# Attention scores from half-array products, two key blocks' tiles at a time

## The chip, the core and the metric

The program runs on one core of a Trainium2 chip. The core has five engines that work through queues of their own in program order and meet at semaphores: TensorE (PE; the loading of its stationary operand is shown apart as PEld), VectorE (DVE), ScalarE (ACT), GpSimd (POOL) and SyncE (SP, which issues most transfers). The metric is the device time of one execution in microseconds, as the median of several. Lower is better.

## The reference, cut to what matters

One layer: a combined input projection of 2048 positions, then dilated attention in three head groups, a gated linear recurrence, two gated output projections, a merge, an output projection and a layer norm. The change lies in the attention.

```python
DILATION_GROUPS = ((128, 1), (512, 4), (2048, 16))     # (window, dilation); 8 heads of 64 each
...
    s = jnp.einsum('brnqhd,brnkhd->brnhqk', qb, kw) * (Dh ** -0.5)
    # query blocks of 128 against [previous block, current block] of keys, banded
    s = jnp.where(valid[None, None, :, None], s, NEG_INF)
    m = jnp.max(s, axis=-1, keepdims=True)
    p = jnp.exp(s - m)
    l = jnp.sum(p, axis=-1, keepdims=True)
    o = jnp.einsum('brnhqk,brnkhd->brnqhd', p, vw)
```

Everything is float32. The kernel multiplies in a reduced float32 type and restores the accuracy by splitting an operand x into a rounded high part and a low part, x - high; a product q k is formed as qh kh + ql kh + qh kl.

## The kernel before, in words

The program has three stages one after the other. The first (to 1464 us of the profiled execution) is the input projection; it writes the rotated queries, already split (`qh`, `ql`), and the keys to scratch in DRAM, channel by channel: 64 channels of one head on 64 partitions. The second (1464 to 1791 us) is the attention. The third is the combination of the groups and the other projections. The order on PE, ACT, DVE, POOL and SP is that in which the Python code emits the instructions; no scheduler moves them.

The attention loop runs over 192 tiles `m`, 16 in each of 12 units `u`. A unit is two heads of one group; the groups alternate in the order 0, 2, 1, dilations 1, 16, 4. A tile is one block of 128 queries for both heads, against one or two blocks of keys: a full tile has two key blocks (256 columns), a narrow one has one (128). Dilation 16 has narrow tiles only, dilation 4 has four narrow ones at the start of a unit, dilation 1 has one.

In step `m` of the loop the code emits three things for three different tiles:

- `step_s(m)`: the scores into PSUM (`s`), then on DVE, for each head, one instruction that adds the mask and takes the minimum (the signs are turned, so the minimum is the greatest score), and on ACT, for each head, the exponential (`p`);
- `step_t(m - 3)`: TensorE transposes the exponentials into PSUM (`pt`), and ACT or, for every third tile, DVE copies them to SBUF (`ptb`);
- `step_v(m - 4)`: TensorE multiplies the copied tile by the values (`o`); after every second tile DVE copies `o` to `osb`, which ACT's queue sends to DRAM.

For the scores, `unit_parts` lays queries and keys out so that 128 rows of the array are used for a head of 64 channels. `A[:, h]` holds the high queries on 64 partitions and the low ones on the other 64; `B1[:, h]` holds the high keys on both halves; `b2[:, h]` holds the low keys on the half of the high queries and zeros on the other. Two products per head then give all three terms. The keys are split on POOL when they have landed: a cast to the high part, a second cast that copies it to the other half, and a subtraction, for each head and each half of the positions (twelve instructions per unit, those of the first keys on ACT and DVE). A unit's keys and queries are asked for from SP during the unit before.

Names in the listings: `A` queries, `B` high keys, `C` keys and then their low part, `V` values, `k_scr`, `qh_scr`, `ql_scr`, `v_scr` the scratch they come from. The weights of the first stage are `l` (low parts, from `wl_scr`).

Of the kernel before, what the change touches and what calls it, by code (L numbers as in the profile page):

```python
# [15 lines left out]
P = 128  # L16
# [15 lines left out]
def hybrid_block_kernel(ctx: ExitStack, tc: tile.TileContext, a: dict, out: bass.AP):  # L32
# [634 lines left out]
    for s in range(1, NQ):  # L667
# [16 lines left out]
        for j in range(7):  # L684
            if plan[s][0] and j % 2 == 0:
                at(t0 + j - 1, lambda s=s, j=j: load_lo(s, j))
            at(t0 + j, lambda s=s, j=j: prep_w(s, j))
# [71 lines left out]
    USLOT = (("X4", "X3", "X2"), ("Y0", "X1", "X0"))  # L759
    VSLOT = {(0, 0): "X5", (2, 0): "Y1", (1, 0): "Y2", (0, 1): "X5", (2, 1): "Y1", (1, 1): "Y2"}  # L760
    zero = [False, False]
    B2 = {}
# [7 lines left out]
    def unit_parts(u):  # L770

        sl = USLOT[u % 2]
        g, hp = unit(u)
        q = {(n, h): qk_scr[n, 4 * g + hp].rearrange("(d h) s -> h d s", h=2)[h] for n in ("qh", "ql", "k") for h in range(2)}

        def k_part(h, hs, os):
            def fn():
                if h == 0:
                    units[u] = [None, big(sl[1], [P, 2, S], F32R, f"B{u}")]
                    if u < 2:  # L780
                        B2[u] = big(sl[2], [P, 2, S], F32R, f"C{u}")
                        pool.memset(flat(B2[u][up_, 0]), 0.0)
                        pool.memset(flat(B2[u][lo_, 1]), 0.0)
                    units[u].append(B2[u % 2])
                _, B1, b2 = units[u]
                sp.dma_start(flat(b2[hs, h]), q["k", h])

                def split(t):
                    if (u, h) == (0, 0):
                        act.activation(B1[hs, h, t], flat(b2[hs, h, t]), AF.Copy)  # L790
                        act.activation(B1[os, h, t], flat(B1[hs, h, t]), AF.Copy)
                        eng = dve
                    else:
                        pool.tensor_copy(B1[hs, h, t], flat(b2[hs, h, t]))
                        pool.tensor_copy(B1[os, h, t], flat(B1[hs, h, t]))
                        eng = pool
                    eng.tensor_tensor(out=b2[hs, h, t], in0=flat(b2[hs, h, t]), in1=flat(B1[hs, h, t]), op=ALU.subtract)  # L797

                later(3, lambda: split(slice(0, S // 2)))
                later(4, lambda: split(slice(S // 2, S)))  # L800
            return fn

        def q_part(hs, h, n):
            def fn():
                if (hs, h) == (lo_, 0):
                    units[u][0] = big(sl[0], [P, 2, S], F32R, f"A{u}")
                sp.dma_start(flat(units[u][0][hs, h]), q[n, h])
            return fn

        return [k_part(0, lo_, up_), k_part(1, up_, lo_), q_part(lo_, 0, "qh"), q_part(up_, 0, "ql"),  # L810
                q_part(lo_, 1, "ql"), q_part(up_, 1, "qh")]
# [66 lines left out]
    first, second, firstv = unit_parts(0), unit_parts(1), v_parts(0, 0)  # L878
    low = NS
    where = [(s, j) for s in range(NQ) for j in range(ticks[s])]  # L880
    for T, (s, j) in enumerate(where):
# [10 lines left out]
        if s == NQ - 1:  # L892
            for fn in ((), (), first[:2], first[2:], firstv, second[:1], second[1:2])[j]:
                fn()
        evacuate(s, j)
# [31 lines left out]
    def step_s(m):  # L927
        u, n = divmod(m, 16)
        g, _ = unit(u)
        A, B1, b2 = units[u]  # L930
        pv = prev(g, n)
        lo = 0 if pv is not None else P
        s = aps.tile([P, 2, 256], F32, tag="s", name=f"s{m}", bufs=3)
        if n % 4 == 0:
            st["osb"] = at_p.tile([P, 4, 132], F32, tag="osb", name=f"osb{m}", bufs=6)
        osb = st["osb"]
        for h in range(2):
            q = A[:, h, n * P:(n + 1) * P]
            for i, B in enumerate((B1, b2)):
                if g == 2:  # L940
                    k = B[:, h].rearrange("p (c r i) -> p r c i", c=4, r=16)[:, max(n - 1, 0):n + 1]
                elif pv is None:
                    k = B[:, h, n * P:(n + 1) * P]
                elif g == 0:
                    k = B[:, h, (n - 1) * P:(n + 1) * P]
                else:
                    c, r = divmod(n, 4)
                    k = B[:, h, (c - 1) * CH:(c + 1) * CH].rearrange("p (c r j) -> p r c j", c=2, r=4)[:, r]
                pe.matmul(s[:, h, (0 if g == 2 and n else lo):256], q, k, start=(i == 0), stop=(i == 1))  # L949
        p = at_p.tile([P, 2, 256], F32, tag="p", name=f"p{m}", bufs=5)  # L950
        for h in range(2):
            mm = osb[:, n % 4, 130 + h:131 + h]
            dve.tensor_tensor_reduce(out=p[:, h, lo:256], in0=s[:, h, lo:256], in1=mask[:, lo:256],  # L953
                                     scale=1.0, scalar=3e38, op0=ALU.add, op1=ALU.min, accum_out=mm)
            act.activation(p[:, h, lo:256], p[:, h, lo:256], AF.Exp, scale=-1.0, bias=mm)  # L955
# [87 lines left out]
    for m in range(NB + 4):  # L1043
        u, n = divmod(m, 16)
        run(late)
        if m < NB:
            step_s(m)
# [342 lines left out]
```

## Time and profile before

| | us |
|---|---|
| median of 3 runs | 2276.87 (2275.35 to 2277.63) |
| the profiled execution | 2272.4 |
| its span, first to last instruction | 2270.6 |
| first stage | 0 to 1464 |
| attention | 1464 to 1791 |
| the rest | 1791 to 2270.6 |

A row of busy time by stretches gives the stretch, its length and then for each engine the microseconds in which it was busy, with the number of instructions, then the granted TensorE clock (1.00 is full speed), the share of the DMA engines and GB/s. A row of the timeline gives start, duration, engine, line, operation, tiles written and read, and in brackets how long the engine had been idle and what ended that. A row of instruction groups gives line, engine, operation, tiles, shapes and count, then busy microseconds and mean nanoseconds of one, then the engine's idle time before them and what ended it. Matmuls overlap, so distances between their starts tell more than their durations.

### The profile page before, as it was taken

How to read it: one execution, taken by the hardware profiler on the slowest of the kernel's cores; microseconds unless marked ns; L12 is line 12 of the kernel's file. 1: busy time of each engine (PE TensorE's matmuls, PEld its weight loads, DVE VectorE, ACT ScalarE, POOL GpSimd, SP SyncE). 2: the span in 40 equal slices, each digit the busy share in tenths (PEclk: the TensorE clock that was granted, in tenths of full speed). 3: DMA queues.
4: the chain of work that ended last, by engine and by line, in shares of the span. 5: the costliest groups of instructions: out<-in, count | busy, mean ns of one | idle time of the engine just before them, and what ended most of it. 6: DMA issues, size and time to landing. Idle time of an engine off the chain costs nothing.

```text
span 2270.6 us, 33643 instructions
## 1 busy us (share of the span) xinstructions
PE 2218.0 (98%) x11032; PEld 1869.3 (82%) x11032; DVE 1748.2 (77%) x3244; ACT 1209.9 (53%) x2161; POOL 821.6 (36%) x606
## 2 busy tenths in 40 slices
PE   8999999999999999999999999989999999989998
PEld 6888888888887888888888888889999877767786
DVE  7888898899888786877888877656666578747677
ACT  5456566666565566766677677556666411221100
POOL 1555455455543001201201200476766156421220
PEclk9999999999999999999999999999999999999999
DMA  6977987977977666666766856996977588764431
GB/s 209 261 230 223 264 234 232 259 225 247 262 236 261 210 192 205 212 181 198 221 198 198 230 174 203 264 243 160 261 181 174 177 278 289 255 209 158 157 121 65
DMA packets 307358, 485.84 MB, mean 214 GB/s; under 512 B 90432, under 2 KB 131424, under 8 KB 302576
## 3 DMA queue, kind: packets, MB, share of 16 engines
q1 hardware_dynamic: 278192, 441.80, 63.1%
q0 software_dynamic: 9888, 17.90, 4.9%
q10 hardware_dynamic: 19104, 23.99, 3.4%
q8 instruction: 88, 1.44, 0.3%
q14 instruction: 86, 0.70, 0.1%
HBM read 305.27 MB, written 178.32 MB: 213 GB/s over the span
## 4 chain that ended last, share of the span: by engine, by line
PE 80%; issue 5%; DMA 5%; DVE 5%; POOL 3%; ACT 2%; SPq 1%; ACTq 0%; DVEq 0%; POOLq 0%
PE q L614 58%; PE o L988 4%; PE s L949 3%; PE yb L1177 2%; PE yb L1178 2%; PE yb L1176 2%; PE pt L964 2%; PE z L1270 1%; PE z L1269 1%; PE z L1268 1%; DMA A<-qh_scr 1%; POOL me L1242 1%; PE vtp L366 1%; DMA ybr<-yb_scr 1%; POOL C L797 1%
## 5 line engine op out<-in xcount | busy, mean ns | idle before, releaser
L614 PE MATMUL q<-xT,hS 128*128 128x512 f32 x1632 | 504.0, 390 | 1.4 <-DVE y L230 1.4
L614 PE MATMUL q<-xB,hA 128*128 128x512 f32 x1344 | 417.4, 392 | 9.5 <-ACT xB L218 8.8
L614 PE MATMUL q<-xT,l 128*128 128x512 f32 x1088 | 423.6, 389 | 0.0
L614 PE MATMUL q<-xB,l 128*128 128x512 f32 x944 | 368.4, 390 | 0.0
L614 PEld LDWEIGHTS q<-xT,hS 128*128 128x128 f32 x1632 | 305.3, 188 | 64.8 <-issue 1.8
L614 PEld LDWEIGHTS q<-xB,hA 128*128 128x128 f32 x1344 | 252.3, 189 | 62.9 <-ACT xB L218 8.8
L614 PEld LDWEIGHTS q<-xT,l 128*128 128x128 f32 x1088 | 204.2, 188 | 42.6
L955 ACT ACTIVATE p<-p,osb 128x256 f32<-128x256 f32 (+1 forms) x384 | 156.4, 454 | 112.4 <-DVE osb L953 109.2
L614 PEld LDWEIGHTS q<-xB,l 128*128 128x128 f32 x944 | 177.7, 188 | 37.2
L953 DVE CUSTOM_DVE_ANT_0 p<-s,mask 128x256 f32<-128x256 f32 (+1 forms) x384 | 125.3, 364 | 97.2 <-PE s L949 63.0
L230 POOL TENSOR_TENSOR sw<-sw,sin 128x512 f32<-128x512 f32 x96 | 154.6, 1632 | 122.6 <-ACT sw L318 99.8
L230 POOL TENSOR_TENSOR y<-y,h 128x512 f32<-128x512 f32 x28 | 40.3, 1440 | 413.7 <-DVE h L517 292.6
L988 PE MATMUL o<-V,ptb 128*128 128x65 f32 x1200 | 165.7, 276 | 9.5 <-ACT ptb L969 7.5
L988 PEld LDWEIGHTS o<-V,ptb 128*128 128x128 f32 x1200 | 152.7, 195 | 20.8 <-ACT ptb L969 18.2
L614 PE MATMUL q<-xB,hS 128*128 128x512 f32 x544 | 168.6, 391 | 0.3 <-DVE v L230 0.3
L614 PE MATMUL q<-xT,hA 128*128 128x512 f32 x544 | 168.2, 390 | 0.1
L274 ACT ACTIVATE hA<-wA 128x512 fp32r<-128x512 f32 x220 | 138.8, 635 | 21.2 <-PE g L483 6.6
L274 ACT ACTIVATE hS<-S 128x512 fp32r<-128x512 f32 x170 | 108.5, 638 | 63.8 <-DVE S L230 56.6
L230 POOL TENSOR_TENSOR l<-wA,hA 128x512 fp32r<-128x512 f32 x68 | 108.5, 1596 | 80.8 <-ACT hA L274 59.2
L949 PE MATMUL s<-B,A 128*128 128x256 f32 (+1 forms) x384 | 116.2, 325 | 4.1 <-DMA A<-qh_scr 2.1
L614 PEld LDWEIGHTS q<-xT,hA 128*128 128x128 f32 x544 | 101.6, 188 | 21.5 <-issue 0.7
L614 PEld LDWEIGHTS q<-xB,hS 128*128 128x128 f32 x544 | 101.3, 188 | 21.3 <-issue 0.7
(196 smaller groups left out, 4923.6 us busy)
## 6 DMA issues: line engine op xcount, KB each, us to landing
wA<-in_w_in_dram SPq DMA_DIRECT2D x219, 256.0 KB, 4.6
wl_scr<-l SPq DMA_DIRECT2D x102, 512.0 KB, 4.6
l<-wl_scr SPq DMA_DIRECT2D x102, 512.0 KB, 4.0
wS<-in_w_in_dram SPq DMA_DIRECT2D x102, 256.0 KB, 4.2
wS<-in_w_in_dram POOLq DMA_DIRECT2D x68, 256.0 KB, 6.8
mg_scr<-y SPq DMA_DIRECT2D x59, 256.0 KB, 5.0
o_scr<-osb ACTq DMA_DIRECT2D x48, 264.0 KB, 6.0
oc<-o_scr SPq DMA_DIRECT2D x48, 264.0 KB, 5.0
```

Source lines behind the costliest of these rows:

```text
L230: eng.tensor_tensor(out=out, in0=in0, in1=in1, op=op)
L274: act.activation(heads(h), heads(r, False), AF.Copy)
L366: pe.transpose(tp[:, b, :], flat(vt)[:, b * P:(b + 1) * P], ident)
L614: pe.matmul(bank, w[:, ks], x[:, kk, xx], start=(first and i == 0), stop=(last and i == 11))
L949: pe.matmul(s[:, h, (0 if g == 2 and n else lo):256], q, k, start=(i == 0), stop=(i == 1))
L953: dve.tensor_tensor_reduce(out=p[:, h, lo:256], in0=s[:, h, lo:256], in1=mask[:, lo:256], scale=1.0, scalar=3e38, op0=ALU.add, op1=ALU.min ...
L955: act.activation(p[:, h, lo:256], p[:, h, lo:256], AF.Exp, scale=-1.0, bias=mm)
L964: pe.transpose(pt[:, 2 * h + x, :], p[:, h, x * P:(x + 1) * P], ident)
L988: pe.matmul(o[:, n % 2, h * 65:h * 65 + 65], ptb[:, 2 * h + x, :], V[:, kb, vo + h * 65:vo + h * 65 + 65], start=(x == lo // P), stop=(x = ...
L1176: pe.matmul(yb, WL[f][:, 0, k], xx[:, 0], start=(k == 0), stop=False)
L1177: pe.matmul(yb, WL[f][:, 0, k], xx[:, 1], start=False, stop=False)
L1178: pe.matmul(yb, WL[f][:, 1, k], xx[:, 0], start=False, stop=(k == 7))
```

## The change

Queries and keys of a unit are held once: `A[:, 0]` the high and `A[:, 1]` the low queries, one head on partitions 0 to 63 and the other on 64 to 127; one tile of high keys, one of low keys, in the same way. A head's scores are three products of 64 rows each (high queries with high keys, high with low, low with high). The two heads' products alternate, and each head writes its own PSUM bank. `step_s` is called for every second `m` and does the tiles `m` and `m + 1`: twelve products, then the four mask-and-minimum instructions and the four exponentials. PSUM now has two banks for each head's scores and two for the transposes, where it had three and three. The keys are split by one cast and one subtraction over 128 partitions for each half of the positions, emitted in steps 1 and 2 of the unit before; queries and keys are asked for two units ahead. In the last projection tiles the keys of unit 1 and the first queries are asked for earlier, and one load of low weights is moved ahead by two ticks.

```diff
-                at(t0 + j - 1, lambda s=s, j=j: load_lo(s, j))
+                at(t0 + (3 if s == NQ - 1 and j == 6 else j - 1), lambda s=s, j=j: load_lo(s, j))
...
+    def k_split(u, x, fast=False):
+        if x == 0:
+            units[u][1] = big(KSLOT[u % 2], [P, S], F32R, f"B{u}")
...
+        lo, hi = piece(units[u][2]), piece(units[u][1])
+        if fast:
+            act.activation(hi, flat(lo), AF.Copy)
+        else:
+            pool.tensor_copy(hi, flat(lo))
+        (dve if fast else pool).tensor_tensor(out=lo, in0=flat(lo), in1=flat(hi), op=ALU.subtract)
...
-    def step_s(m):
-        u, n = divmod(m, 16)
+    def step_s(m0):
+        u, n0 = divmod(m0, 16)
...
-        s = aps.tile([P, 2, 256], F32, tag="s", name=f"s{m}", bufs=3)
...
-            for i, B in enumerate((B1, b2)):
...
-                pe.matmul(s[:, h, (0 if g == 2 and n else lo):256], q, k, start=(i == 0), stop=(i == 1))
+        bank = [aps.tile([P, 2, 256], F32, tag=f"s{h}", name=f"s{h}{m0}", bufs=2) for h in range(2)]
+        todo = []
+        for b in range(2):
+            n = n0 + b
...
+            for i, (x, B) in enumerate(((0, hi), (0, low), (1, hi))):
+                for h, hs in enumerate((lo_, up_)):
...
+                    pe.matmul(bank[h][:, b, (0 if g == 2 and n else lo):256], A[hs, x, n * P:(n + 1) * P], k,
+                              start=(i == 0), stop=(i == 2))
+            todo.append((m0 + b, lo))
+        for m, lo in todo:
...
+            p = at_p.tile([P, 2, 256], F32, tag="p", name=f"p{m}", bufs=6)
...
-        pt = aps.tile([P, 4, P], F32, tag="t", name=f"pt{m}", bufs=3)
+        pt = aps.tile([P, 4, P], F32, tag="t", name=f"pt{m}", bufs=2)
...
-        if m < NB:
+        if m < NB and m % 2 == 0:
             step_s(m)
         if 3 <= m < NB + 3:
             step_t(m - 3)
         if m >= 4:
             step_v(m - 4)
-        if n == 0 and 1 <= u <= 10:
-            loads += unit_parts(u + 1)
+        if 1 <= n <= 2 and u <= 10:
+            k_split(u + 1, n - 1)
+        if n == 0 and 1 <= u <= 9:
+            loads += k_parts(u + 2)
+        if n == 0 and u <= 9:
+            loads += q_parts(u + 2)
```

What this does to the order is shown at three places. First TensorE in unit 0, around the transposes of tiles 9 and 10. The number in a name is the tile's: `pt9` and `ptb9` are the transposed tile 9, `s13` the scores of tile 13 (of both heads); in the new kernel `s012` and `s112` are the scores of heads 0 and 1 for tiles 12 and 13. The last number is the buffer's. Before:

```order
L964 MATMUL pt9_14355<-ident_163,p9_14281 128x128 x4
L988 MATMUL o8_14362<-V00_14021,ptb8_14333 128x65 x4
L949 MATMUL s13_14368<-B0_13978,A0_14001 128x256
L949 MATMUL s13_14368<-C0_13979,A0_14001 128x256
L949 MATMUL s13_14368<-B0_13978,A0_14001 128x256
L949 MATMUL s13_14368<-C0_13979,A0_14001 128x256
L964 MATMUL pt10_14378<-ident_163,p10_14304 128x128 x4
L988 MATMUL o8_14362<-V00_14021,ptb9_14356 128x65 x4
```

And now, from the last four of the twelve score products of tiles 12 and 13:

```order
L954 MATMUL s012_14355<-C0_13942,A0_13962 128x256
L954 MATMUL s112_14356<-C0_13942,A0_13962 128x256
L954 MATMUL s012_14355<-B0_14005,A0_13962 128x256
L954 MATMUL s112_14356<-B0_14005,A0_13962 128x256
L976 MATMUL pt9_14380<-ident_163,p9_14274 128x128 x4
L1000 MATMUL o8_14387<-V00_14023,ptb8_14344 128x65 x4
L976 MATMUL pt10_14393<-ident_163,p10_14320 128x128 x4
L1000 MATMUL o8_14387<-V00_14023,ptb9_14381 128x65 x4
L954 MATMUL s014_14405<-B0_14005,A0_13962 128x256
L954 MATMUL s114_14406<-B0_14005,A0_13962 128x256
```

Between the transposes `pt9` and the products that read their copy `ptb9` stood a tile's scores, and now none stands there; the next scores come behind both.

Second ACT, at the same place; `p` are the exponentials (x2 for the two heads), `ptb` the copies that fall to ACT. Before:

```order
L955 ACTIVATE p12_14350<-p12_14350,osb12_14345 128x256 x2
L1002 DMA o_scr00_58<-osb4_14163 128x4x132
L955 ACTIVATE p13_14373<-p13_14373,osb12_14345 128x256 x2
L969 ACTIVATE ptb10_14379<-pt10_14378 128x512
L955 ACTIVATE p14_14395<-p14_14395,osb12_14345 128x256 x2
L969 ACTIVATE ptb11_14401<-pt11_14400 128x512
L955 ACTIVATE p15_14417<-p15_14417,osb12_14345 128x256 x2
```

And now:

```order
L967 ACTIVATE p12_14370<-p12_14370,osb12_14369 128x256 x2
L967 ACTIVATE p13_14375<-p13_14375,osb12_14369 128x256 x2
L1014 DMA o_scr00_58<-osb4_14171 128x4x132
L981 ACTIVATE ptb10_14394<-pt10_14393 128x512
L967 ACTIVATE p14_14419<-p14_14419,osb12_14369 128x256 x2
L967 ACTIVATE p15_14424<-p15_14424,osb12_14369 128x256 x2
L981 ACTIVATE ptb11_14430<-pt11_14429 128x512
```

The copy `ptb11` stood behind the exponentials of tile 14 and ahead of those of 15; now it stands behind both.

Third SP, at the end of the first stage; `A0` and `A1` are the queries of units 0 and 1, `V00` and `V20` the first values of groups 0 and 2. Before:

```order
L786 DMA C0_13979<-k_scr0_82 64x2048 x2
L807 DMA A0_14001<-qh_scr0_80 64x2048
L807 DMA A0_14001<-ql_scr0_81 64x2048 x2
L807 DMA A0_14001<-qh_scr0_80 64x2048
L824 DMA V00_14021<-v_scr00_74 128x4x260 x4
L786 DMA C1_14050<-k_scr8_106 64x2048 x2
L807 DMA A1_14106<-qh_scr8_104 64x2048
L807 DMA A1_14106<-ql_scr8_105 64x2048 x2
```

And now:

```order
L780 DMA C0_13942<-k_scr0_82 64x2048 x2
L811 DMA A0_13962<-qh_scr0_80 64x2048 x2
L811 DMA A0_13962<-ql_scr0_81 64x2048 x2
L780 DMA C0_13942<-k_scr8_106 64x2048 x2
L827 DMA V00_14023<-v_scr00_74 128x4x260 x4
L811 DMA A1_14080<-qh_scr8_104 64x2048 x2
L811 DMA A1_14080<-ql_scr8_105 64x2048 x2
```

The keys of unit 1 are asked for ahead of the first values, where they stood behind them.

112 lines of the change are left out of this document (51 added, 61 removed).

## Prediction

> **What bounds the kernel now.** I read the page first, then the busy time by stretches, then the timeline of single tiles in the attention stage, because the diff touches nothing else but the asking of its first loads.
>
> ```profile
> PE 2218.0 (98%) x11032; PEld 1869.3 (82%) x11032; DVE 1748.2 (77%) x3244; ACT 1209.9 (53%) x2161; POOL 821.6 (36%) x606
> 1464.00:1791.00 327.00, 311.37 (x2559) 299.70 (x2558) 200.35 (x936) 211.42 (x521) 208.47 (x143) 0.97 0.76 200
> 1548.80:1578.10 29.30, 29.05 (x253) 28.36 (x252) 18.43 (x78) 19.54 (x44) 17.68 (x12) 1.00 0.58 145
> 1578.10:1600.40 22.30, 21.81 (x184) 20.86 (x184) 13.52 (x77) 13.97 (x42) 17.66 (x12) 1.00 0.97 234
> 1600.40:1626.10 25.70, 25.05 (x212) 23.79 (x212) 16.99 (x81) 18.02 (x45) 17.63 (x12) 1.00 0.99 294
> ```
>
> The rows are stretches: length, busy time of PE, PEld, DVE, ACT and POOL, granted clock, DMA. TensorE carries the program (98%), and the attention stage is 327 us of it. The last three rows are units 3, 4 and 5, one of each dilation (1, 16, 4), each from its first score product to the next unit's. TensorE is busy for 29.05 of 29.30 us while DVE, ACT and POOL have 18.43, 19.54 and 17.68: in the undisturbed units TensorE is the bound. Four rounds of these three make 4 x 77.3 = 309.2 us; the rest of the 327 is stalls and the ends.
>
> Now one full tile (two key blocks) in the timeline; columns are start, duration, engine, line, operation.
>
> ```profile
> 1474.45 0.69 DVE L971 COPY ptb<-pt 128x512 f32<-128x512 f32 x1
> 1474.78 0.36 PE L949 MATMUL s<-B,A 128*128 128x256 f32 x1
> 1474.98 0.28 PE L949 MATMUL s<-C,A 128*128 128x256 f32 x1
> 1475.22 0.28 PE L949 MATMUL s<-C,A 128*128 128x256 f32 x1
> 1475.34 0.60 PE L964 MATMUL pt<-ident,p 128*128 128x128 f32 x4
> 1475.65 0.42 DVE L953 CUSTOM_DVE_ANT_0 p<-s,mask 128x256 f32<-128x256 f32 x1 [0.51 <-PE s L949]
> 1475.78 1.00 PE L988 MATMUL o<-V,ptb 128*128 128x65 f32 x8
> 1476.00 0.42 DVE L953 CUSTOM_DVE_ANT_0 p<-s,mask 128x256 f32<-128x256 f32 x1
> 1476.12 0.91 ACT L955 ACTIVATE p<-p,osb 128x256 f32<-128x256 f32 x2 [0.98 <-DVE osb L953]
> 1476.59 0.36 PE L949 MATMUL s<-B,A 128*128 128x256 f32 x1
> 1476.93 0.58 ACT L969 ACTIVATE ptb<-pt 128x512 f32<-128x512 f32 x1
> 1477.58 1.08 PE L988 MATMUL o<-V,ptb 128*128 128x65 f32 x8
> 1478.47 0.36 PE L949 MATMUL s<-B,A 128*128 128x256 f32 x1
> ```
>
> Scores start at 1474.78, 1476.59, 1478.47: a tile lasts 1.81 or 1.88 us, a pair 3.69. In it TensorE issues 4 score products (0.20 to the second, then 0.12 each), 4 transposes (1475.34 to 1475.78, 0.44) and 8 value products (0.81 or 0.89). A step costs 0.10 to 0.12 whether 256, 128 or 65 columns stream. The other half of the reading is the chain that returns to TensorE: the last score product starts at 1475.22, the first mask-and-minimum 0.43 later, the second after another 0.35, the first exponential 0.47 after the first minimum, two exponentials take 0.91, and only then ACT copies the transposed tile (1476.93 to 1477.51); the value products that read it start at 1477.58. So already now the copy is finished 0.07 before its use. The chain is nearly as long as the work that covers it, because between a tile's transposes and its value products TensorE has a whole other tile to do.
>
> In narrow tiles (one key block) the cover is shorter and the chain is visible:
>
> ```profile
> 1507.95 0.42 DVE L971 COPY ptb<-pt 128x256 f32<-128x256 f32 x1
> 1508.20 0.36 PE L949 MATMUL s<-B,A 128*128 128x256 f32 x1
> 1508.63 0.28 PE L949 MATMUL s<-C,A 128*128 128x256 f32 x1
> 1509.06 0.29 DVE L953 CUSTOM_DVE_ANT_0 p<-s,mask 128x128 f32<-128x128 f32 x1 [0.20 <-PE s L949]
> 1509.28 0.29 DVE L953 CUSTOM_DVE_ANT_0 p<-s,mask 128x128 f32<-128x128 f32 x1
> 1509.40 0.69 ACT L955 ACTIVATE p<-p,osb 128x128 f32<-128x128 f32 x2 [0.84 <-DVE osb L953]
> 1510.00 0.36 ACT L969 ACTIVATE ptb<-pt 128x256 f32<-128x256 f32 x1
> 1510.41 0.52 PEld L988 LDWEIGHTS o<-V,ptb 128*128 128x128 f32 x4 [0.36 <-ACT ptb L969]
> 1510.88 0.36 PE L949 MATMUL s<-B,A 128*128 128x256 f32 x1
> ```
>
> From the last score product to the minimum 0.43, to the exponential 0.34, two exponentials 0.60, the copy 0.36, and the value products' weight load has waited 0.36 for that copy; scores follow 0.47 after.
>
> **The change part by part.**
>
> *Order on the queues.* Scores come for two tiles at once, ahead of the two tiles' transposes and value products. TensorE's queue per pair is now 12 score products, transposes of tile m-3, values of m-4, transposes of m-2, values of m-3. ACT's queue per pair is the four exponentials of m and m+1, then the copy of m-3, then that of m-2 (DVE has every third copy, behind four minima). The values of m-3, which stand ahead of the next scores, thus need a copy that stands behind all the exponentials of this pair's scores. Before, that copy had until after the next tile's scores; now only the values of m-4 and the transposes of m-2 lie between. What is queued behind the waiting value product on TensorE is everything, the next scores among it, so the chain closes into a loop per pair. Its length, in full tiles, with the two heads' products side by side (six steps):
>
> - scores: the last pair of products issues at 0.20 + 4 x 0.12 = 0.68 (both heads' minima need the bank's last product, the second tile's);
> - first minimum 0.43 later, 1.11; first exponential 0.47 later, 1.58;
> - four exponentials at 0.455: 3.40 (the minima, 0.35 apart, keep ahead); copy 0.58: 3.98; the weight load 0.05 later (0.41 from the narrow copy's start, less its 0.36): 4.03;
> - eight value products, 0.85 in the mean: the next scores at 4.88.
>
> Where DVE has the copy: 1.11 + 4 x 0.35 = 2.51, copy 0.69, values at 3.20, scores at 4.05. TensorE itself reaches those values at 0.80 + 0.44 + 0.85 + 0.44 = 2.53 (0.80 is 0.20 and five steps) and waits. Two pairs in three copy on ACT: (2 x 4.88 + 4.05) / 3 = 4.60 against 3.69. Narrow: 0.68 + 0.43 + 0.34 + 1.20 + 0.41 + 0.47 = 3.53; with DVE 1.11 + 4 x 0.22 + 0.42 + 0.05 + 0.47 = 2.93; mean 3.33.
>
> How many of each:
>
> ```profile
> L955 ACT ACTIVATE p<-p,osb 128x256 f32<-128x256 f32 x216 | 97.8, 501 | 59.9 <-DVE osb L953 59.9
> L955 ACT ACTIVATE p<-p,osb 128x128 f32<-128x128 f32 x168 | 58.6, 395 | 52.5 <-DVE osb L953 49.2 <-DMA o_scr<-osb 2.5
> L797 POOL TENSOR_TENSOR C<-C,B 64x1024 fp32r<-64x1024 f32 x45 | 106.5, 2366 | 3.2
> L794 POOL CAST B<-C 64x1024 fp32r<-64x1024 f32 x45 | 46.6, 1035 | 87.1 <-DMA C<-k_scr 72.0 <-PE pt L964 9.5 <-PE s L949 4.8
> ```
>
> 216 exponentials over two key blocks are 108 full tiles, 54 pairs; 168 are 84 narrow ones, 42 pairs (a mixed pair counts half to each). The stage's units become 54 x 4.60 + 42 x 3.33 = 388.3 instead of 309.2: **+79.1**. TensorE's own saving, two of eight steps a pair and one of two slow first steps, lies inside the wait and is worth nothing by itself.
>
> *Half-array products.* Every row above has 128 rows of array; none has 64. Bounds: six steps a pair if the heads' products and their weight loads run side by side, twelve if each takes a step of its own, 6 x 0.12 = 0.72 a pair more, 69 over 96 pairs, all on the loop since scores open it. I take six: two heads write two banks and use disjoint rows, so nothing in the rows makes one wait for the other; the steps that cost the same at 65 and at 256 columns speak for a step being a weight load, and so for twelve. Both ends stay. [...]
>
> Changing between 64 and 128 rows happens twice a pair, and only the change into the scores is on the loop. [...]
>
> *Keys and queries.* POOL's work of a unit was four rounds of two casts and a subtraction, 4 x (1.04 + 1.04 + 2.37) = 17.8; it becomes two of a cast and a subtraction over 128 partitions, 6.8 if time goes by columns, 13.6 if by elements: under the unit's 22 us and more either way, off the loop. Loads keep their count (two of k, four of q), a unit earlier on SP's queue; unit 1's keys pass the first values, which no product reads before the fifth step. What they remove are the waits at the stage's front:
>
> ```profile
> 1466.25 0.30 PE L949 MATMUL s<-B,A 128*128 128x128 f32 x1 [2.13 <-DMA A<-qh_scr]
> 1491.30:1523.10 31.80, 25.28 (x185) 23.87 (x184) 13.59 (x77) 14.07 (x42) 17.80 (x14) 0.89 0.85 240
> 1493.65 0.33 PE L949 MATMUL s<-B,A 128*128 128x128 f32 x1 [1.95 <-POOL B L795]
> 1496.07 0.47 PE L949 MATMUL s<-C,A 128*128 128x128 f32 x1 [2.08 <-POOL C L797]
> ```
>
> Unit 1 takes 31.8 where unit 4, of its kind, takes 22.3: 9.5, waits for POOL of 1.95 and 2.08 and a halved clock after them. With the 2.13 before the first scores **-11.6**; at least the 6.2 of bare waits goes, at most that 11.6 and some clock. The last low weights, asked two ticks earlier, and the splits of unit 0 on ACT and DVE lie under the last projection's products. Transposes have two banks for three: the bank's earlier copy is one that the value products just ahead have waited for, nothing. The tail's weight splits on ACT and DVE in unit 11 now lie on the loop: 0 to +7.
>
> Sum against the profiled execution: 2272.4 + 79.1 - 11.6 = 2339.9. That execution lies 4.5 under the median of the runs (2276.87), so 2344 on that scale.
>
> **The rivals.**
>
> *One after the other.* The halves don't overlap (the change doesn't do what it says): +69, 2413. Decided by the step between score products.
>
> *TensorE stays the bound* (the other side). If the copy got ahead of the exponentials, so that the loop were under TensorE's own 0.80 + 2 x (0.44 + 0.85) = 3.38 a pair, 3.69 - 3.38 = 0.31 a pair would be won: 96 x 0.31 = 30, with the front's 11.6: 2235. It needs 1.5 less than the 4.88 above. For it: 1.00 clock and 98% busy now. Against it: the narrow tiles, whose 0.37 wait is this chain with two exponentials, and this, in unit 11:
>
> ```profile
> 1759.49 1.29 DVE L1017 SCALAR_TENSOR_TENSOR wl<-wlr,wl 128x512 fp32r<-128x512 f32 x2 [0.40 <-ACT wl L1016]
> 1762.04 1.12 PE L988 MATMUL o<-V,ptb 128*128 128x65 f32 x4 [1.85 <-ACT ptb L969]
> 1512.29:1515.70 3.41, 1.84 (x16) 1.59 (x15) 1.73 (x10) 0.95 (x4) 3.35 (x3) 1.00 0.48 121
> 1758.05:1761.46 3.41, 2.14 (x20) 1.90 (x18) 2.76 (x12) 2.17 (x6) 0.00 (x0) 1.00 0.23 80
> 1761.46:1771.70 10.24, 9.56 (x43) 9.16 (x44) 6.40 (x26) 7.02 (x17) 3.38 (x3) 0.50 0.47 155
> ```
>
> Two weight splits (1.29 on DVE) stood ahead of the minima, the copy came later by as much, and TensorE waited 1.85.
>
> *The loop, and a halved clock.* After that wait the clock stood at 0.50 for 10.24 us. The stretch before had PE busy for 2.14 of 3.41; another with 1.84 of 3.41 kept the full clock. The loop's waits of 1.5 in 4.9 lie near that. At half clock, with steps taken as twice as long, a full pair's loop gains 6 x 0.12 in scores and 0.85 in values, 1.6, a narrow one's 0.72 + 0.47 = 1.2: a quarter of all pairs gives (54 x 1.6 + 42 x 1.2) / 4 = 34, 2378; all give 2481.
>
> **How the numbers follow.** The loop with heads side by side 0.55; one after the other 0.25; loop with clock losses 0.08; TensorE still the bound 0.09; gains and wait cancelling 0.03. Range 2300 to 2425: it takes in the loop, the serial case and most of the clock's, and leaves out the two cases on the fast side and the far end of the clock's. A change under 0.2%, about 4.5 us, can't be told from none. Slower 0.88, same 0.03, faster 0.09.
>
> **What would show it.** Right: value products that wait about 1.5 us for ACT's copy in two pairs of three and 0.7 for DVE's, units of about 37 us (8 x 4.60), 27 (8 x 3.33) and 34 (6 x 4.60 + 2 x 3.33) for dilation 1, 16 and 4, score products of two heads starting together, unit 1 without waits for POOL. Wrong: score products 0.12 apart twelve times (serial), TensorE without waits between transposes and values (no loop), or clock rows under 0.9 across the stage.

## The result, and the profile after

The changed kernel takes 2403.11 us in the median (2384.62 to 2445.07), the kernel before, beside it on the same chip, 2277.25 (2275.35 to 2279.47): a ratio of 1.053, 95% interval 1.049 to 1.057. Forecast was slower by 67 us; it is slower by 126. The profiled execution took 2390.76 us; the runs spread with the granted clock over the span, 0.928 to 0.965 in the four of the changed kernel, and a ratio leaves out the runs of a kernel that are over 1.5% above its shortest, while a median takes them all. All of the loss lies in the attention stage: what is ahead of it ends 2 us earlier, what is behind it takes 481 us for 480. First the page (busy time, and the granted clock in 40 slices, which was 9 in all of them before):

```profile
PE 2288.5 (96%) x11416; PEld 1906.9 (80%) x11416; DVE 1746.2 (73%) x3244; ACT 1199.4 (50%) x2159; POOL 685.2 (29%) x508
PEclk9999999999999999999999998897687899999999
```

Then the stretches: the stage, unit 1, units 3 and 4, and one stretch at half clock in units 5 and 6.

```profile
1462.00:1908.00 446.00, 384.48 (x2965) 339.40 (x2965) 197.69 (x937) 204.19 (x523) 84.15 (x52) 0.82 0.56 150
1500.20:1531.20 31.00, 23.34 (x215) 19.80 (x214) 12.92 (x77) 13.82 (x43) 10.91 (x7) 0.98 0.99 252
1568.70:1606.20 37.50, 31.91 (x283) 28.15 (x282) 18.51 (x78) 18.36 (x42) 6.75 (x5) 0.95 0.36 88
1606.20:1634.80 28.60, 22.84 (x215) 19.33 (x214) 12.98 (x77) 13.70 (x43) 4.87 (x4) 1.00 0.94 244
1639.40:1714.50 75.10, 73.86 (x398) 67.95 (x396) 27.39 (x121) 27.65 (x65) 7.12 (x5) 0.50 0.53 150
```

The stage went from 327 to 446 us. Unit 3 has TensorE busy for 31.91 of 37.50 us, where unit 3 before had 29.05 of 29.30: TensorE now waits in every pair of this unit. And for 75.10 us TensorE is busy nearly throughout (73.86) at a clock of 0.50. The stage's clock is 0.82; before it was 0.97. Under 0.9 across the stage was one of the prediction's signs of being wrong, and it has come.

The timeline of one pair whose awaited copy is ACT's, and the end of the next, whose copy is DVE's:

```profile
1592.23 0.39 PE L954 MATMUL s<-B,A 64*128 64x256 f32 x2
1592.45 0.28 PE L954 MATMUL s<-C,A 64*128 64x256 f32 x2
1592.92 0.28 PE L954 MATMUL s<-B,A 64*128 64x256 f32 x2
1593.35 0.42 DVE L965 CUSTOM_DVE_ANT_0 p<-s,mask 128x256 f32<-128x256 f32 x1 [0.58 <-PE s L954]
1593.82 1.71 ACT L967 ACTIVATE p<-p,osb 128x256 f32<-128x256 f32 x4 [2.67 <-DVE osb L965]
1595.43 1.05 ACT L981 ACTIVATE ptb<-pt 128x512 f32<-128x512 f32 x2
1596.05 1.11 PE L1000 MATMUL o<-V,ptb 128*128 128x65 f32 x8 [0.98 <-ACT ptb L981]
1597.09 0.39 PE L954 MATMUL s<-B,A 64*128 64x256 f32 x2
1599.57 0.69 DVE L983 COPY ptb<-pt 128x512 f32<-128x512 f32 x1
1600.31 1.11 PE L1000 MATMUL o<-V,ptb 128*128 128x65 f32 x8 [0.38 <-DVE ptb L983]
1601.35 0.39 PE L954 MATMUL s<-B,A 64*128 64x256 f32 x2
```

This is the predicted loop: scores, minima, four exponentials, the copy, the value products that waited 0.98 for it, the next scores. From scores to scores it is 4.86 us (forecast 4.88) and 4.26 (4.05). The waits are shorter than forecast, 0.98 and 0.38 for 1.5 and 0.7, since TensorE's own part of a pair is longer than forecast (3.61 for 3.38, as the first experiment shows) and ACT's copy comes 0.2 earlier. The wait that ends this loop, in the stage (total, times, longest):

```profile
PE o L1000 <- ACT ptb L981: 47.5, 54, 2.3
```

At the front, POOL's waits are gone and another has come. Of SyncE's queue, one wait:

```profile
SPq L780 <- DMA mg_scr<-y: 10.3, 1, 10.3
```

And the timeline there, SyncE's issues and the first value products:

```profile
1461.79 1.08 SPq L780 DMA_DIRECT2D C<-k_scr  x2
1462.98 4.54 SPq L827 DMA_DIRECT2D V<-v_scr  x4
1472.21 1.09 PE L1000 MATMUL o<-V,ptb 128*128 128x65 f32 x4 [5.47 <-DMA V<-v_scr]
```

Unit 1's keys waited 10.3 us at the head of SyncE's queue, the first values were asked for behind them, at 1462.98 and not at 1457.00 as before, and TensorE waited 5.47 for them. Unit 1 takes 31.0 us, as it did before (31.8), without any wait for POOL.

### The profile page after: what moved, and what is told of

It is laid out like the page before. It is cut to its first block, busy times and chain, and to the rows that moved or that the text cites. A ratio compares the mean times of both kernels' runs of the same rounds, so it can differ in the third digit from the quotient of the medians.

```text
span 2389.0 us, 34159 instructions
## 1 busy us (share of the span) xinstructions
PE 2288.5 (96%) x11416; PEld 1906.9 (80%) x11416; DVE 1746.2 (73%) x3244; ACT 1199.4 (50%) x2159; POOL 685.2 (29%) x508
## 4 chain that ended last, share of the span: by engine, by line
PE 79%; DVE 6%; DMA 5%; issue 4%; ACT 4%; POOL 1%; SPq 0%; ACTq 0%; DVEq 0%; POOLq 0%
PE q L614 55%; PE o L1000 5%; PE s L954 4%; ACT p L967 2%; PE z L1286 2%; PE z L1284 2%; PE z L1285 2%; DVE p L965 2%; PE yb L1193 1%; PE yb L1194 1%; PE yb L1192 1%; PE pt L976 1%; PE vtp L366 1%; ACT ptb L981 1%; DMA o_scr<-osb 1%
## 5 line engine op out<-in xcount | busy, mean ns | idle before, releaser
L1000 PE MATMUL o<-V,ptb 128*128 128x65 f32 x1200 | 196.5, 310 | 60.9 <-ACT ptb L981 47.5
L967 ACT ACTIVATE p<-p,osb 128x256 f32<-128x256 f32 (+1 forms) x384 | 145.6, 450 | 216.6 <-DVE osb L965 216.6
L1000 PEld LDWEIGHTS o<-V,ptb 128*128 128x128 f32 x1200 | 183.2, 229 | 82.7 <-ACT ptb L981 62.5
L965 DVE CUSTOM_DVE_ANT_0 p<-s,mask 128x256 f32<-128x256 f32 (+1 forms) x384 | 117.7, 362 | 71.0 <-PE s L954 69.3
L1004 DVE COPY osb<-o 128x260 f32<-128x260 f32 x96 | 41.2, 429 | 161.4 <-PE o L1000 161.4
L976 PE MATMUL pt<-ident,p 128*128 128x128 f32 x600 | 123.8, 326 | 0.0
L799 POOL CAST B<-C 128x1024 fp32r<-128x1024 f32 x22 | 22.8, 1037 | 336.5 <-PE s L954 269.5
```

What stands on the lines that cost most here:

```text
L965: dve.tensor_tensor_reduce(out=p[:, h, lo:256], in0=bank[h][:, m % 2, lo:256], in1=mask[:, lo:256], scale=1.0, scalar=3e38, op0=ALU.add, o ...
L976: pe.transpose(pt[:, 2 * h + x, :], p[:, h, x * P:(x + 1) * P], ident)
L1000: pe.matmul(o[:, n % 2, h * 65:h * 65 + 65], ptb[:, 2 * h + x, :], V[:, kb, vo + h * 65:vo + h * 65 + 65], start=(x == lo // P), stop=(x = ...
L1004: dve.tensor_copy(osb[:, b:b + 2, 0:130], o)
```

## The experiments

Each is read against the kernel before, run beside it on the same chip (2274 to 2276 us).

**One step more between transposes and value products.** Undoes the loop and leaves everything else.

```diff
-        ptb = at_p.tile([P, 4, P], F32, tag="pt", name=f"ptb{m}", bufs=3)
+        ptb = at_p.tile([P, 4, P], F32, tag="pt", name=f"ptb{m}", bufs=4)
...
-    for m in range(NB + 4):
+    for m in range(NB + 5):
...
-        if m >= 4:
-            step_v(m - 4)
+        if m >= 5:
+            step_v(m - 5)
```

> The changed kernel with one edit: the value products of a tile stand one step later (five steps behind its scores and not four, with four ptb buffers for three), so that between the copy of a pair's transposes and the value products that read it there is a whole step more. Theory (the loop through ScalarE's copy: a pair's transposes, four exponentials, the copy, the value products, the next pair's scores): TensorE no longer waits for the copy; a full pair goes from 4.86/4.27 us to what TensorE itself does, 3.3 to 3.5, a narrow one from 3.64/3.03 to 2.1 to 2.4; the waits of the value products for ACT's copy, 47.5 + 62.5 us on PE and its weight loads, fall under 20; the granted clock of the attention stage rises from 0.82 to 0.95 or more. Time 2235 to 2275 us, below the kernel before. Rival 1 (the half-array products or the two changes of array mode per pair are what costs): pairs stay at 4.2 us or more and the time at 2340 or more. Rival 2 (ScalarE is the next bound, with four exponentials of 0.42 us and two copies in three per pair): full pairs of 3.7 to 4.0, 2290 to 2320.

Measured: 2260.97 us, ratio to before 0.996 (0.994 to 0.998). Units 3, 4 and 5:

```profile
1561.50:1589.70 28.20, 28.20 (x283) 26.60 (x282) 18.02 (x78) 18.80 (x44) 6.69 (x5) 1.00 0.77 184
1589.70:1611.00 21.30, 21.30 (x221) 19.64 (x220) 11.92 (x78) 13.16 (x42) 5.49 (x5) 1.00 0.86 215
1611.00:1634.30 23.30, 23.21 (x239) 21.65 (x238) 16.43 (x79) 17.22 (x46) 8.04 (x5) 1.00 0.92 251
```

And the group of the value products in the stage, with its idle time and what ended it:

```profile
L1000 PE MATMUL o<-V,ptb 128*128 128x65 f32 x1200 | 163.9, 276 | 4.4 <-DMA V<-v_scr 4.4
```

TensorE is busy all of the time in these units, the copy ends no wait of the value products any more (the 4.4 us left are for the first values), full pairs take 3.61 us and narrow ones 2.30. The loop theory holds and both rivals fall; the loop with all that hangs on it is worth what lies between this kernel and the changed one, 130 us by the two ratios and 142 by the medians. TensorE's own pair is 3.61 and not the 3.38 of the prediction, nor the 3.3 to 3.5 expected here. The clock falls short too: 0.92 in the stage, where 0.95 was expected, with 37.5 us at half clock behind a pair of 9.91 us in unit 1. This profile is of the longest of the ten runs (2277.46; the shortest is 2257.37).

**The same step in the kernel before.** The same two edits, on the kernel with 128-row products.

> The kernel before with its value products one step later (five steps behind the scores, four ptb buffers), as the first experiment did to the changed kernel: what of that one's gain is the step alone. Theory: the full tiles are bound by TensorE and stay at 1.81 us, the narrow ones, which go 1.14 and 1.54 by turns because of the copy, go to 1.15; some 20 tiles of 48 per group of three units save up to 0.39: units 3, 4, 5 from 77.3 to 72 to 75 us, 2252 to 2265 in all. Rival (the copy is not what the narrow tiles wait for): 2270 to 2280.

Measured: 2261.90 us, ratio 0.994 (0.993 to 0.996).

```profile
1551.10:1579.30 28.20, 28.20 (x252) 28.20 (x252) 18.42 (x78) 19.61 (x45) 17.67 (x12) 1.00 0.62 153
1579.30:1600.50 21.20, 21.20 (x189) 21.20 (x188) 13.47 (x77) 13.99 (x42) 16.82 (x12) 1.00 0.95 223
1600.50:1623.60 23.10, 23.10 (x208) 23.10 (x208) 17.06 (x79) 17.78 (x45) 14.17 (x11) 1.00 1.03 295
```

Unit for unit this is the kernel above: 72.5 us for three units against 72.8. So away from the front nothing of the gain over the kernel before (77.3 us) is owed to the half-array products; all of it is the step, which frees the tiles from the copy.

**Two tiles at a time in the kernel before.** One part of the change alone: `step_s` issues the products of m and m+1 and then their softmax; 128-row products and the old front stay.

```diff
-    def step_s(m):
+    def step_s(m0):
+        todo = [products(m) for m in (m0, m0 + 1)]
+        for x in todo:
+            softmax(*x)
...
-        if m < NB:
+        if m < NB and m % 2 == 0:
             step_s(m)
```

> The kernel before (128-row score products with the zero-filled keys, its front and its buffers for q and k) with one part of the change alone: the scores of two tiles are asked for at once, four score banks, two transpose banks, six p buffers. Theory (the loop through the copy comes from two tiles at a time, whatever the products): full pairs of 4.4 to 4.7 us where ACT copies and 3.8 to 4.1 where DVE does, narrow ones near 3.1 to 3.5, TensorE waiting for the copy as in the changed kernel; +50 to +80 us by the loop, and up to 45 more where the clock halves: 2325 to 2400. Rival (the half-array products cost the time): no change, 2270 to 2285.

Measured: 2317.01 us (2314.39 to 2323.14), ratio 1.019 (1.017 to 1.021): +42.6, a little under the theory's +50, and not the rival's nothing. Units 3 and 4:

```profile
1555.50:1589.50 34.00, 29.90 (x252) 28.00 (x251) 18.65 (x78) 18.65 (x42) 17.66 (x12) 1.00 0.50 124
1589.50:1615.60 26.10, 22.32 (x186) 20.61 (x184) 13.46 (x77) 13.99 (x43) 17.61 (x12) 1.00 0.88 230
```

One pair in the timeline: the first score product, the first minimum, the value products that waited for ACT's copy, the next scores.

```profile
1572.17 0.36 PE L954 MATMUL s<-B,A 128*128 128x256 f32 x1
1573.01 0.42 DVE L962 CUSTOM_DVE_ANT_0 p<-s,mask 128x256 f32<-128x256 f32 x1 [0.19 <-PE s L954]
1575.73 1.11 PE L997 MATMUL o<-V,ptb 128*128 128x65 f32 x8 [0.66 <-ACT ptb L978]
1576.64 0.36 PE L954 MATMUL s<-B,A 128*128 128x256 f32 x1
```

The loop comes from two tiles at a time, whatever the products: 4.47 to 4.50 us a pair (3.90 where DVE copies). Beside the changed kernel's 4.86 it shows what the half-array products add inside the loop: from the first score product to the first minimum 0.84 against 1.12 (1.11 in the forecast), since a bank that holds one head of both tiles is complete only with the last of twelve products, and from the values to the scores 0.91 against 1.04. In all a pair whose copy is ACT's is 0.36 to 0.39 longer. And TensorE's value products wait here as in the changed kernel, 45.6 us in 57 waits for ACT's copies against 47.5 in 54, yet the clock over the profiled span is 0.992.

**TensorE kept busy in the wait.** The changed kernel, with transposes issued again while the copy is awaited.

```diff
+        again = (2 if lo else 1) * 2 if m % 2 == 0 and (m - 1) % 3 else 0
+        for _ in range(1 + again):
```

> The changed kernel with work added: in the pairs whose awaited copy is ScalarE's, the transposes of the next tile are issued three times (five times where it is narrow) and not once, the same values over the same bank, so that TensorE is busy for 0.9 us of the 1.5 that it else waits for the copy. Theory on the clock (the granted clock halves over stretches of 75 us and less because TensorE waits so often and so long in this loop): pairs of 4.9 to 5.1 us at full clock, hardly any at 6.7, granted clock of the attention stage from 0.82 to 0.95 or more: 2345 to 2380 us, shorter than the changed kernel with more work. Rival 1 (the clock falls for another cause, as total work or power): clock as low or lower, 2400 or more. Rival 2 (the added transposes delay the copy, which waits for the bank's last transposes): pairs of 5.7, 2440 or more whatever the clock.

Measured: 2362.86 us (2357.60 to 2366.02), ratio 1.038 (1.036 to 1.040): 40 us shorter than the changed kernel, with 512 transposes more.

```profile
1462.90:1888.00 425.10, 389.98 (x3486) 348.83 (x3486) 198.35 (x937) 207.37 (x527) 84.24 (x52) 0.96 0.59 157
1578.00:1615.10 37.10, 34.67 (x323) 31.16 (x322) 18.51 (x78) 18.48 (x42) 6.73 (x5) 1.00 0.36 87
1615.10:1644.00 28.90, 27.04 (x257) 23.74 (x256) 13.10 (x77) 13.96 (x43) 4.98 (x4) 1.00 0.95 240
1644.00:1677.70 33.70, 31.02 (x291) 27.60 (x290) 16.84 (x77) 17.30 (x43) 8.52 (x6) 1.00 0.59 173
```

The pairs are as long as in the changed kernel (4.86 and 4.28), the stage's clock rises from 0.82 to 0.96. So at least 35 to 40 us (by the ratios, by the medians) are the clock's, for 34 us of this stage are still at half clock, and at most 86 to 88 the loop's with the front. Both rivals fall.

**One tile at a time, half-array products kept.**

```diff
-        for b in range(2):
+        for b in range(1):
...
-        if m < NB and m % 2 == 0:
+        if m < NB:
             step_s(m)
```

> The changed kernel with one part undone: the scores of one tile are asked for at a time, with the half-array products, the two banks by heads and the new front kept. Theory (two tiles at a time make the loop): TensorE has no wait for the copy beyond 0.3 us a tile, a full tile takes 1.7 to 1.95 us with one change of array mode and back per tile and not per pair, clock 0.95 or more; 2250 to 2295. Rival (half-array products or mode changes cost the time): with twice as many mode changes the stage is as long as in the changed kernel or longer, 2390 or more; in between, each 100 ns that a mode change costs is 150 changes more, +15 to +20 us.

Measured: 2331.35, 2350.95, 2370.16 and 2396.91 us; the ratio, of the first two, is 1.029 (1.024 to 1.034), about 2341 us, between the expectations. Units 3, 4 and 5, and a stretch behind the wait for the first values:

```profile
1590.20:1621.40 31.20, 31.20 (x285) 27.82 (x284) 18.83 (x78) 19.80 (x44) 6.76 (x5) 1.00 0.58 133
1621.40:1645.10 23.70, 23.70 (x215) 20.31 (x214) 13.58 (x78) 13.92 (x42) 6.12 (x4) 1.00 0.89 222
1645.10:1672.10 27.00, 26.84 (x243) 23.36 (x242) 16.85 (x77) 18.06 (x45) 7.33 (x6) 1.00 0.94 274
1473.00:1575.40 102.40, 102.15 (x525) 90.38 (x526) 36.97 (x174) 36.15 (x94) 20.25 (x12) 0.50 0.67 172
```

TensorE never waits, as the loop theory says, but at full clock three units take 81.9 us against 72.8 with two tiles at a time: 24 rounds of changes more, 0.38 us for each. And behind that wait the clock stays at 0.50 for 102 us with TensorE busy for 102.15 of them. That is not the story of waits which I had for the clock.

**The change of rows by itself.** The kernel before with one product of 4 columns per tile ahead of its scores, on 64 rows in one kernel and on 128 in the other.

```diff
+        pe.matmul(s[:, 0, 252:256], A[0:64, 0, n * P:(n + 1) * P], B1[0:64, 0, n * P:n * P + 4],
+                  start=True, stop=True)
```

> The kernel before with one product more per tile: 64 rows, 4 columns, into the score bank just ahead of the tile's score products, which write over it. So TensorE goes from 128 rows to 64 and back once a tile, for nearly no columns. Read against the same kernel with a 128-row product in that place. Theory (the change of rows and back costs about 0.35 us, from 3.96 us for two tiles with two such changes against 3.61 with one): 0.3 to 0.35 us a tile more than the 128-row one, +50 to +67 us over 192 tiles. Rival (it costs less than 0.1 us, and the 0.35 is from the half-array products themselves): under +20. On the clock, after the wait of 7.5 us at the start of unit 1: if the changes of rows keep the granted clock low, it stays at 0.50 for tens of us; if it is the columns streamed through half the rows, it is back after 7 to 10 us as in the kernel before.

> The kernel before with one product more per tile, 128 rows and 4 columns, into the score bank just ahead of the tile's score products: what a weight load of 128 columns and a short product cost without a change of rows. Expected by both theories: 0.05 to 0.2 us a tile where TensorE is the bound, +8 to +35 us: 2282 to 2310.

Measured: ratio 1.0255 (1.0235 to 1.0276) with 64 rows, 1.008 (1.005 to 1.011) with 128. The four runs with 64 rows took 2331.52, 2336.26, 2473.90 and 2525.43 us, at a clock over the span of 0.984, 0.983, 0.921 and 0.899; the ratio is of the first two. The profile is of the last, and is read for the steps of a tile at full clock and for what the clock does. A tile with the 64-row product in the timeline, to the next one's:

```profile
1486.14 0.27 PE L937 MATMUL s<-B,A 64*128 64x4 f32 x1
1486.34 0.39 PE L951 MATMUL s<-B,A 128*128 128x256 f32 x1
1488.28 0.27 PE L937 MATMUL s<-B,A 64*128 64x4 f32 x1
```

The same with the 128-row product:

```profile
1480.75 0.25 PE L937 MATMUL s<-B,A 128*128 128x4 f32 x1
1480.86 0.37 PE L951 MATMUL s<-B,A 128*128 128x256 f32 x1
1482.68 0.25 PE L937 MATMUL s<-B,A 128*128 128x4 f32 x1
```

And the longest stretch at half clock with 64 rows:

```profile
1517.20:1943.90 426.70, 426.70 (x1842) 409.50 (x1841) 135.61 (x619) 138.32 (x341) 149.34 (x102) 0.50 0.38 97
```

A full tile is 2.14 us with the 64-row product and 1.93 with the 128-row one: a change and back costs 0.21, half on the way in (the values' last product to the probe 0.21, where a step is 0.11) and half on the way out (0.20 against 0.11). Over 192 tiles that is 40 us, and so are the 1.7% between the two ratios: no rival case, but less than the theory's 50 to 67. The 0.38 above has more in it, of which I can name 0.10, the slow first step of each run of products (0.22 for 0.12); 0.07 stay open. With 64 rows the halved clock stayed for 427 us of a TensorE that was never idle; with 128 the longest such stretch was 20.5 us. But the two shorter runs with 64 rows have nearly the clock of those with 128 (0.985 to 0.989), so such a stretch doesn't come each time.

**First values ahead of unit 1's keys**, on the kernel with the step added:

```diff
-    begin = {0: k_parts(0), 1: q_parts(0), 2: k_parts(1), 4: firstv[:1], 5: firstv[1:]}
+    begin = {0: k_parts(0), 1: q_parts(0), 4: firstv[:1], 5: firstv[1:] + k_parts(1)}
```

> The changed kernel with the value products one step later (as in the first experiment) and a second edit: SyncE asks for the first values ahead of unit 1's keys, not behind them. Theory (the wait of unit 1's keys for a transfer of mg_scr, with the values queued behind it, made the first values late): the pair of 7.5 us in unit 0 shrinks to 4.5 or less, the wait of the value products for V from 4.4 us to under 1.5; 2250 to 2258 us against 2261 of the first experiment. A second stall of 9.9 us in unit 1 (ScalarE's issue of o_scr waits for its own earlier transfer, exponentials behind it) should stay, and the halved clock behind it. Rival (the values arrive no earlier, since all 16 DMA engines are busy then, or unit 1's keys now come late): 2260 or more, with a wait of the same size at V or at the first products of unit 1.

Measured: 2257.45 us, ratio 0.992 (0.990 to 0.993). The 7.51 us pair of unit 0 is 2.67, unit 0 takes 24.6 us and not 30.4. The second stall, expected to stay at ScalarE's o_scr, became a wait of 2.1 us for unit 2's queries, with 17 us of halved clock behind it.

**o_scr on GpSimd's queue**, on top of that, and in the 128-row kernel with the step:

```diff
-            later(2, lambda: act.dma_start(dst, osb))
+            later(2, lambda: pool.dma_start(dst, osb))
```

> The changed kernel with its value products one step later, the first values ahead of unit 1's keys, and a third edit: the transfers of the finished rows to o_scr are issued by GpSimd's queue and not by ScalarE's. In the run with the first two edits a transfer to o_scr of 17 us (1475.7 to 1492.9) held SyncE's next load back for 12 us, which came to the same completion slot; the queries of unit 2 came 2.1 us late and the clock stood at 0.50 for 17 us behind that. Theory: SyncE's loads are then 5 us or more earlier, no wait for the queries of unit 2, unit 2 of 33.6 us goes to 24 or 25; 2244 to 2252 us against 2257. Rival (the DMA engines' bandwidth alone sets when the queries of unit 2 land, or GpSimd's queue is late with o_scr because it waits for keys to split): 2255 or more.

> The kernel before with its value products one step later and o_scr on GpSimd's queue: the same help for the kernel with 128-row products, to see what the half-array products bring in the best form of either. Units 3, 4, 5 stood at 28.2, 21.2 and 23.1 us with 128-row products and a step more, at 28.3, 21.2 and 23.3 with half-array ones, so that nothing but the front can differ. Theory (GpSimd splits the keys of a unit in 17.8 us here and in 6.8 there; its waits for keys lie ahead of o_scr): the front gains less than 5 us; 2257 to 2264, some 10 above the other. Rival (the front's waits come from the slots of o_scr here too): 2245 to 2252, no difference between the two forms.

Measured: 2250.62 us, ratio 0.989 (0.987 to 0.991), for the half-array kernel, the shortest of all here (unit 2 takes 23.4 us and not 33.6, unit 1 now 26.0 for 22.0); 2282.52, ratio 1.003 (1.001 to 1.004), for the 128-row one. The second is longer than any expectation. Its row, the minimum that has to wait for the transfer of rows it will write over:

```profile
1614.67 0.42 DVE L953 CUSTOM_DVE_ANT_0 p<-s,mask 128x256 f32<-128x256 f32 x1 [7.70 <-DMA o_scr<-osb]
```

GpSimd's queue has 17.8 us of splits per unit there and issues o_scr behind them: ahead of this wait it split keys from 1585.07 on, then issued four transfers of o_scr together, from 1603.25 to 1605.10, and they took 13.7 us in the median to land. In the whole stage the minima wait 24.7 us for o_scr there (three waits), and 2.0 (one) with 6.8 us of splits. So in these kernels what the change brings of lasting worth is the keys held once: a POOL queue with room.

**Head after head.** The order of the twelve products, on the kernel with both the step and the first values ahead.

```diff
-            for i, (x, B) in enumerate(((0, hi), (0, low), (1, hi))):
-                for h, hs in enumerate((lo_, up_)):
+            for h, hs in enumerate((lo_, up_)):
+                for i, (x, B) in enumerate(((0, hi), (0, low), (1, hi))):
```

> The changed kernel with the value products one step later and the first values ahead of unit 1's keys, and the six half-array products of a tile in another order: three of the first head, then three of the second, and not by turns. It tells what it is worth that the two heads' products lie on different rows of the array. Theory (they run side by side only where neighbours lie on different rows; the pairs start 0.12 us apart): twelve steps of 0.11 to 0.12 us for six per pair of tiles, +0.6 to +0.75 us per full pair, so 4.2 to 4.35 against 3.61, and 2.9 to 3.0 against 2.30 for a narrow one; +55 to +70 us, 2312 to 2330, with no more halved clock than without. Rival (the array takes them in any order at the same rate): 2250 to 2265.

Measured: 2256.38 us against 2257.45, pairs of 3.62: no difference, my theory wrong. The score products of a pair:

```profile
1560.83 0.39 PE L954 MATMUL s<-B,A 64*128 64x256 f32 x2
1561.06 0.29 PE L954 MATMUL s<-C,A 64*128 64x256 f32 x2
1561.18 0.40 PE L954 MATMUL s<-B,A 64*128 64x256 f32 x4
1561.52 0.29 PE L954 MATMUL s<-B,A 64*128 64x256 f32 x2
```

They still start two by two, six steps, though three of one head now stand ahead of the other's: in program order a product of B is followed by one of C, and here two of B start at 1560.83 and two of C at 1561.06. By this trace products on the other rows overtake, and TensorE's queue does not keep to the program's order there.

## Why the prediction was right, and where not

The forecast of +67 was 59 us short of the +126: 35 to 40 of them are the clock's, 11.6 the front's, some ten the loop's. The median lies in the range, towards its upper end, because the range took in other cases than the one that was forecast.

*The loop (+79.1)* was right in kind and nearly in size. At full clock three units of the changed kernel, as the filled one shows them undisturbed, take 37.1 + 28.9 + 33.7 = 99.7 us against 77.3, four times 22.4 is 89.6. The ten us too little are the changes between 64 and 128 rows, for which the sum has no term: values to scores take 1.04 and not 0.85 to 0.91. In ACT's pairs it did not show because four exponentials take 1.61 and not 1.82 (1593.82 to 1595.43), so that 4.86 beside 4.88 is luck; in DVE's pairs, which have no such offset, it did, 4.26 for 4.05. That the exponentials are shorter stood in the prediction's own rows: from the first of two at 1476.12 to the copy at 1476.93 are 0.81 us, and the 0.91 that it used holds an overlap. The steps in the experiment with 64-row probes put 0.10 us on each change (0.20 to 0.21 where a step is 0.11); how it comes about was not shown.

*Heads side by side (six steps)* was right, against the rival of twelve that I had given 0.25: 0.11 to 0.12 between pairs of products. In the changed kernel's trace the two heads' products start 3 ns apart in the median of 390 at full clock, and 20 ns at most.

*The clock* is the step of the prediction that failed in size. "The loop, and a halved clock" had a chance of 0.08 and +34 for a quarter of the pairs; 35 to 40 us came in fact, in a stage with 160 us of its 446 at half clock (9 stretches; before 3, with 20 us). I had read its chance from the length of the waits alone. The runs show a second condition: two tiles at a time with 128-row products has nearly the same waits (TensorE is busy for 0.88 of unit 3 there, for 0.85 in the changed kernel) and the clock holds (0.98 in the stage, where the changed kernel has 0.82); with half-array products the full clock came back late in three of eight kernels, even where TensorE does not wait. In the changed kernel and with one tile at a time all four runs have a low clock over the span, 0.928 to 0.969. In the kernel before, the stage's three stretches at 0.50 lasted 3.41, 6.83 and 10.24 us, with TensorE busy for 3.41, 5.98 and 9.56 of them. With half-array products the clock was not always back so soon: with one tile at a time TensorE was busy for 102.15 us of 102.40 at 0.50. The probe of 4 columns speaks for the changes of rows, and not the columns, as the cause, but its evidence is one profile of a long run, and even the 128-row probe stayed halved for 20.5 us. What keeps the clock halved stays open: a kernel with half rows and no changes of rows was not tried, since this kernel's transposes and value products have all 128.

*The front (-11.6)* was not won. "Unit 1's keys pass the first values, which no product reads before the fifth step" is the sentence that failed: the keys waited 10.3 us for a transfer of mg_scr and the values stood behind them. And with loads asked for a unit ahead the DMA engines are full (a share of 0.99 in unit 1, 0.85 before), and ScalarE's own issue of o_scr waits for its earlier transfer (1510.42 to 1528.65) and holds up the copy: a pair of 5.40 us in unit 1 of the changed kernel, and one of 9.91 with the step added. The changed kernel's row:

```profile
1529.11 0.38 ACT L981 ACTIVATE ptb<-pt 128x256 f32<-128x256 f32 x1 [3.90 <-DMA o_scr<-osb]
```

*TensorE stays the bound (2235)* asked for a loop shorter than TensorE's own pair. With the step added it is, and that pair is 3.61, not 3.38: two changes of rows, 0.2 in all, are in it. Against 128-row products (3.62) nothing is left of the two steps saved. *Off the loop*: POOL's 6.8 us a unit (6.75), the bank of transposes and the splits of unit 0 were as costed.

## What to carry to other kernels

When work is grouped to save engine time, count what stands between a producer and its reader on every queue, not only the time saved: twice the tiles at a time wants a step more of distance, here one buffer against 130 us and more. Two changes of array rows cost as much here (0.2 us) as two steps of products (0.22 to 0.24), so half-array products saved nothing; over longer runs of them they might, which was not tried. And in three of the eight kernels that have them a stall was followed by 75 us and more at half clock. Before loads are moved ahead, look at what each one waits for at the head of its queue, and who stands behind it.

## What was not expected of the hardware

- A change from 128 to 64 rows or back takes about 0.10 us of TensorE (0.205 and 0.20 between starts, where 0.11 is a step).
- The halved clock stayed for 75, 106 and 427 us in the profiles of three kernels with such changes (the changed kernel, one tile at a time, the 64-row probe), with TensorE hardly idle in them; in five more with them the longest stretch was 7 to 38 us (17.0 with the first values ahead, 37.5 in the first experiment). In the five kernels without them it was 7 to 20.5 (10.2 in the kernel before, 20.5 with the 128-row probe).
- With head after head, a product on the other 64 rows starts together with one that stands three places ahead of it in the program (two at 1560.83, the next two at 1561.06).
- A transfer of finished rows to o_scr took 18.2 us in the changed kernel (1510.42 to 1528.65), with the DMA engines at a share of 1.03 meanwhile; the median of its stage is 2.8. And SyncE's queue stood for 11.7 us, until such a transfer, issued by ScalarE, had landed (1481.31 to 1492.98): its next issue, of keys, has the same semaphore for its landing.
